# Attention on one Trainium2 core: the third tile's exponentials multiplied by ScalarE instead of VectorE

## The chip, the core and the metric

The kernel runs on one core of one Trainium2 chip. A core has engines that work side by side, each through a queue of its own in order: TensorE (PE in the profile, with its weight loads as PEld), VectorE (DVE), ScalarE (ACT), GpSimd (POOL) and SyncE (SP), which here issues the loads. The time is the device time of one execution in microseconds (us). Three executions of the kernel before took 1632.38 to 1636.96 us, with a median of 1633.7 us.

## The reference

The kernel computes a two-layer transformer block in float32 on 256 latent tokens and 256 context tokens of width 1024: a half feed-forward, a mixer and another half feed-forward in each layer. The first layer's mixer is attention with 8 query heads and 2 key and value heads of width 128, the second layer's is an mLSTM. The change touches the attention alone:

```python
def gqa_softmax(q, k, v):
    s = jnp.einsum('bqhgd,bkhd->bhgqk', q, k).astype(jnp.float32) * (ATT_HEAD_DIM ** -0.5)
    p = jax.nn.softmax(s, axis=-1).astype(v.dtype)
    return jnp.einsum('bhgqk,bkhd->bqhgd', p, v)
...
    k_all = jnp.concatenate([kl, kc], axis=1)
    v_all = jnp.concatenate([vl, vc], axis=1)
    ...
    ob = lax.map(lambda qblk: gqa_softmax(qblk, k_all, v_all), qb)
    ...
        oc = gqa_softmax(qc.reshape(B, Lc, ATT_KV_HEADS, ATT_GROUP, ATT_HEAD_DIM), kc, vc)
```

Latent queries see all 512 keys; context queries see the 256 context keys only. The softmax divides each row of exponentials by its sum. That division is what the change moves.

## The kernel before

All products of float32 are made from split operands. `split` (line 223) makes a high part by a cast on ScalarE (line 224) and a low part by a subtraction on VectorE (line 229), and `mm3` (line 238) makes three matmuls of them, high by high, high by low and low by high (line 240). So nearly everything that PE multiplies has passed ScalarE and then VectorE.

The program runs stage after stage: the first feed-forward, attention, the second feed-forward, the second layer's feed-forward, the mLSTM and the last feed-forward. In `attention` (line 932) the queries, keys and values are first projected (`part`, with the matmuls of lines 926 to 928), normalised (`evac`, line 956) and turned by transposes on PE (`turn`, line 975). Then a loop of 24 sub-steps runs over the 8 heads and three tiles of a head (line 1128). Tiles 0 and 1 are 128 latent queries each against all 512 keys. Tile 2, the "third tile", holds both blocks of 128 context queries, each against 256 keys, side by side in one tile of 128x512. In each sub-step `scores` makes the scores on PE, a minimum of each row on VectorE (line 1021; the query gain carries a minus sign, so it serves as the maximum), the exponentials with their sums on ScalarE (line 1024), the reciprocals of the sums on VectorE (line 1028), and the product of exponentials and reciprocals (lines 1029 to 1034). Tiles 0 and 1 have one exponential and one product of 128x512 each; the third tile has two of 128x256.

```python
                V.reciprocal(rs, sm)
                for j in range(n):
                    ej = e[:, j * w_ : (j + 1) * w_]
                    if SCALE[i] == "scalar":
                        S.activation(ej, ej, AF.Copy, scale=rs[:, j : j + 1])
                    else:
                        getattr(nc, SCALE[i]).tensor_scalar(ej, ej, rs[:, j : j + 1], None, ALU.mult)
```

`SCALE` (line 69) names the engine for each of the three tiles; before, it is GpSimd, VectorE and VectorE. Three sub-steps later (`AHEAD`, line 61) `values` (line 1037) transposes the scaled tile on PE in four blocks into PSUM (line 1041), splits the transposed tile, and, with the third tile, makes the head's product with the values and splits that as well. The PSUM tiles of these transposes come from a pool of two, which the splits set free. Query heads are split a head ahead (`queries`, line 1004). Between sub-steps `rest` (line 1117) and the loop's end put in the remaining query projections of the context tokens, turns of query blocks (lines 983 to 998), the weights of the output projection, and from sub-step 20 on its first products (`mix_unit`, line 900, with its sum on line 915).

The order of the instructions in each engine's queue is not that of the program text. A planner sets it when the program is built, from the dependencies, the free buffers, the place in the text as priority, and a time that it assumes for each instruction. Only instructions under `pin` keep their order among each other, such as the transposes of lines 983 and 1041. Once built, the queues are fixed and run in order.

## Time and profile before

| what | us |
|---|---|
| median of three executions | 1633.7 |
| lowest and highest | 1632.38, 1636.96 |
| the profiled execution, whole | 1633.42 |
| the profiled execution, its span | 1631.6 |
| attention's sub-steps, first exponential to last | 452 to 520 |
| PE, VectorE, ScalarE, GpSimd busy over the span | 1610.0, 1350.8, 748.9, 62.0 |

The span runs from the first to the last instruction of the profiled execution; the rest of its time lies around it. A row of a group gives the line, engine, operation and shapes, the number of instructions, their busy time and mean duration in nanoseconds, and the idle time of the engine just before them with what ended it. A row of the order in time gives the start and the duration in microseconds, how many instructions of one kind were merged, and in brackets the idle time before and its releaser. Ends of matmuls are modelled, so that a PE shown as busy is not PE at its peak.

### The profile page before, as it was taken

Reading aid. Unit: us, or ns where it says so; the run is one execution under the profiler, and the core shown is the slowest. Engines: PE = TensorE matmul, PEld = TensorE weight load, DVE = VectorE, ACT = ScalarE, POOL = GpSimd, SP = SyncE. Lnnn points to the kernel's source line nnn. Section 1 sums busy time; section 2 is a strip of 40 time slices with the busy share of each in tenths; the row PEclk is TensorE's granted clock in tenths of the full one; section 3 lists DMA queues with packets and bytes.
Section 4 is the critical chain, followed back from the end, with each engine's and each line's share of the span. In section 5 each row is a group of like instructions: output and inputs, shape, how many; then the busy total and the mean of one; then the engine's idle time right before and its main releaser. Section 6 shows DMA issues by size and latency. Waiting matters only on the chain. (4 is left out here: it accounts for less than half of the span.)

```text
span 1631.6 us, 26590 instructions
## 1 busy us (share of the span) xinstructions
PE 1610.0 (99%) x10308; PEld 1448.8 (89%) x10308; DVE 1350.8 (83%) x2689; ACT 748.9 (46%) x1273; POOL 62.0 (4%) x76
## 2 busy tenths in 40 slices
PE   9999999999999999999999999999999999999998
PEld 6888888889988998889998998889999989999987
DVE  5899977739889879899986979789966968897687
ACT  5622122314676453316662434236652657566542
POOL 0000000001011100000000100000001000020000
PEclk9999999999999999999999999999999999999999
DMA  9677765422202347633345248723362332427552
GB/s 367 220 233 244 239 200 194 142 78 85 65 1 76 145 134 219 220 125 104 121 148 184 78 157 286 249 66 120 104 223 100 98 130 84 145 100 258 181 177 91
DMA packets 72495, 252.59 MB, mean 155 GB/s; under 512 B 7984, under 2 KB 10800, under 8 KB 72368
## 3 DMA queue, kind: packets, MB, share of 16 engines
q1 hardware_dynamic: 71792, 250.10, 46.5%
q8 instruction: 81, 1.33, 0.3%
q10 hardware_dynamic: 576, 0.79, 0.1%
q14 instruction: 46, 0.38, 0.1%
HBM read 249.81 MB, written 1.05 MB: 154 GB/s over the span
## 5 line engine op out<-in xcount | busy, mean ns | idle before, releaser
L240 PE MATMUL t<-t,t 128*128 128x256 f32 (+2 forms) x8412 | 1316.5, 317 | 6.4 <-ACT t L224 3.3
L240 PEld LDWEIGHTS t<-t,t 128*128 128x128 f32 x8412 | 1185.2, 188 | 125.6 <-ACT t L224 5.0
L224 ACT CAST t<-t 128x1024 fp32r<-128x1024 f32 (+3 forms) x521 | 428.6, 844 | 488.9 <-PE t L240 215.8
L229 DVE TENSOR_TENSOR t<-t,t 128x256 fp32r<-128x256 f32 (+2 forms) x740 | 514.0, 729 | 114.1 <-ACT t L224 108.0
L340 DVE SCALAR_TENSOR_TENSOR t<-t,t 128x1024 bf16<-128x1024 f32 x224 | 260.7, 1220 | 0.0
L578 ACT ACTIVATE t<-t 128x512 f32<-128x512 f32 (+1 forms) x71 | 34.4, 489 | 107.1 <-PE t L240 107.1
L926 PE MATMUL t<-t,t 128*128 128x256 f32 (+1 forms) x256 | 79.3, 310 | 0.0
L708 DVE SCALAR_TENSOR_TENSOR t<-t,t,t 128x256 f32<-128x256 f32 x96 | 42.7, 478 | 43.9 <-PE t L240 43.6
L927 PE MATMUL t<-t,t 128*128 128x256 f32 (+1 forms) x256 | 78.4, 306 | 0.1
L928 PE MATMUL t<-t,t 128*128 128x256 f32 (+1 forms) x256 | 78.5, 307 | 0.0
L579 DVE TENSOR_TENSOR t<-t,t 128x512 f32<-128x512 f32 (+1 forms) x71 | 39.0, 553 | 44.1 <-PE t L240 30.8
L474 POOL TENSOR_TENSOR t<-t,t 128x256 f32<-128x256 f32 x30 | 23.3, 775 | 1111.4 <-ACT t L464 1110.0
L1441 PE MATMUL t<-t,t 128*128 128x512 f32 (+3 forms) x286 | 60.4, 366 | 1.7 <-ACT t L1518 1.0
L854 PE MATMUL t<-t,t 128*128 128x512 f32 (+1 forms) x300 | 60.5, 364 | 0.0
L1441 PEld LDWEIGHTS t<-t,t 128*128 128x128 f32 (+2 forms) x286 | 43.7, 159 | 18.6 <-issue 2.8
L854 PEld LDWEIGHTS t<-t,t 128*128 128x128 f32 x300 | 51.5, 189 | 8.9
L464 ACT ACTIVATE t<-t 128x256 f32<-128x256 f32 x72 | 26.1, 412 | 65.6 <-DVE t L457 65.6
L927 PEld LDWEIGHTS t<-t,t 128*128 128x128 f32 x256 | 48.1, 188 | 3.3 <-DVE t L229 0.8
L926 PEld LDWEIGHTS t<-t,t 128*128 128x128 f32 x256 | 48.3, 189 | 2.7
L928 PEld LDWEIGHTS t<-t,t 128*128 128x128 f32 x256 | 48.1, 188 | 2.5
L631 DVE TENSOR_TENSOR t<-t,t 128x512 f32<-128x512 f32 x66 | 45.3, 687 | 0.4
L531 ACT ACTIVATE t<-t,t 128x256 fp32r<-128x256 f32 x72 | 32.8, 503 | 27.7 <-DVE t L530 27.7
(201 smaller groups left out, 1069.5 us busy)
## 6 DMA issues: line engine op xcount, KB each, us to landing
t<-in_ffn_in SPq DMA_DIRECT2D x168, 512.0 KB, 4.0
t<-in_ada_w SPq DMA_DIRECT2D x137, 512.0 KB, 4.3
t<-in_ffn_out SPq DMA_DIRECT2D x66, 512.0 KB, 4.4
t<-in_ffn_last SPq DMA_DIRECT2D x22, 512.0 KB, 3.5
t<-in_att_in SPq DMA_DIRECT2D x12, 512.0 KB, 3.5
t<-in_c SPq DMA_DIRECT2D x8, 512.0 KB, 8.0
t<-in_att_out SPq DMA_DIRECT2D x8, 512.0 KB, 3.6
t<-in_ml_qk SPq DMA_DIRECT2D x8, 512.0 KB, 3.8
```

The costliest lines, as they stand in the source:

```text
L224: self.behind(self.nc.scalar.copy(h, x))
L229: self.behind(self.nc.vector.tensor_tensor(out=ls, in0=xs, in1=hs.bitcast(F32), op=ALU.subtract))
L240: mm = lambda *k, **kw: self.nc.tensor.matmul(*k, skip_group_check=not group, **kw)
L340: ins = nc.vector.scalar_tensor_tensor(self.tmp().bitcast(BF16), r, 1.0, self.cb[:, v, :], ALU.mult, ALU.mult, accum_out=to)
L579: V.tensor_tensor(out=sl, in0=sl, in1=pu[:, :n], op=ALU.mult)
L631: add = lambda o, x, y: V.tensor_tensor(out=o, in0=x, in1=y, op=ALU.add)
L708: V.scalar_tensor_tensor(z, y[:, gg[0] - t0 : gg[1] - t0], gate()[:, v, d : d + 1], z, ALU.mult, ALU.add)
L854: pin(nc.tensor.matmul(o, gs[g], ws[k][w][:, i : i + n], start=k == k0 and g == w == 0, stop=k == k1 - 1 and g == 1,))
L926: mm(o, self.xh[:, k, c], wh, start=k == 0, stop=False)
L927: mm(o, self.xh[:, k, c], wl, start=False, stop=False)
L928: mm(o, self.xl[:, k, c], wh, start=False, stop=k == ND - 1)
L1441: mm = lambda *k, **kw: pin(nc.tensor.matmul(*k, **kw))
```

## The change

For the third tile of each head, ScalarE's copy with a scale takes the place of VectorE's multiplication by a scalar: sixteen instructions of 128x256, two to each of eight heads. They read the same exponentials, take the same reciprocals and write to the same place. The branch for it is in `scores` already (line 1031), so that one constant is all that differs:

```diff
@@ -66,7 +66,7 @@
 APD = (4, 5, 6, 7)
 APA = (0, 1, 2, 3, 4, 5, 6, 7)
 QB = 2
-SCALE = ('gpsimd', 'vector', 'vector')
+SCALE = ('gpsimd', 'vector', 'scalar')
 FINE = 4
 FINE0 = 1
```

## The prediction

> **What bounds the kernel now.** I read the head of the page first, then the stretches of the attention stage, then the groups of that stage by shape, and at last the engines' own rows in order of time around each head. From the page, the span and the busy shares:

> ```profile
> span 1631.6 us, 26590 instructions
> PE 1610.0 (99%) x10308; PEld 1448.8 (89%) x10308; DVE 1350.8 (83%) x2689; ACT 748.9 (46%) x1273; POOL 62.0 (4%) x76
> ```

> PE is busy for 99% of the span, so over the whole kernel little but PE's own work sets the time. The change touches one stage only. The stretches of ten microseconds there (columns: length, then busy time and instructions of PE, PEld, DVE, ACT, POOL, then clock, DMA share, GB/s):

> ```profile
> 460.00:470.00 10.00, 8.84 (x67) 8.05 (x66) 9.11 (x25) 6.37 (x20) 1.56 (x1) 1.00 0.00 1
> 480.00:490.00 10.00, 8.37 (x57) 6.95 (x56) 9.54 (x21) 6.55 (x16) 3.12 (x2) 1.00 0.00 0
> 490.00:500.00 10.00, 8.23 (x65) 7.67 (x63) 9.17 (x22) 7.19 (x20) 1.57 (x1) 1.00 0.01 2
> 500.00:510.00 10.00, 8.93 (x60) 7.83 (x59) 9.68 (x21) 7.28 (x18) 1.57 (x1) 1.00 0.31 103
> 510.00:520.00 10.00, 10.00 (x60) 8.75 (x60) 9.13 (x18) 6.20 (x14) 1.57 (x1) 1.00 0.34 109
> ```

> From 460 to 510 VectorE is busy for 9.1 to 9.7 of every 10 us, ScalarE for 6.4 to 7.3, and PE is short of full; from 510 on PE is full. So up to 510 VectorE looks like the limit, and afterwards PE is. How much PE loses is in the groups of the stretch 455 to 531 (last columns: idle time before them, and who ended it):

> ```profile
> L240 PE MATMUL t<-t,t 128*128 128x256 f32 x186 | 27.8, 288 | 4.3 <-ACT t L224 3.1 <-DVE t L229 1.2
> L1041 PE MATMUL t<-t,t 128*128 128x128 f32 x96 | 14.6, 275 | 2.0 <-DVE t L229 1.7 <-ACT t L998 0.2
> L224 ACT CAST t<-t 128x512 fp32r<-128x512 f32 x37 | 21.2, 598 | 14.3 <-PE t L1041 8.7 <-PE t L240 5.6
> L1024 ACT ACTIVATE t<-t,t 128x256 f32<-128x256 f32 x16 | 7.5, 476 | 4.7 <-DVE t L1021 4.7
> ```

> PE stands idle for 4.3 + 2.0 = 6.3 us in these groups. That bounds any ordinary gain: not 0.4% of the time. The first two rows also say that VectorE, though the fuller queue, is not the only one that PE waits for: 3.1 + 0.2 us end with ScalarE (the high part of a split, line 224, or line 998), 1.2 + 1.7 us with VectorE (the low part, line 229). The third row shows ScalarE waiting for PE in turn. It is a round trip, PE (scores or transposes) to ScalarE (high part) to VectorE (low part) to PE, and a delay on either engine counts if it lies on it.

> **The change, part by part.** *Removed from VectorE.* The 16 multiplications of the third tiles, two to each of 8 heads:

> ```profile
> L1034 DVE TENSOR_SCALAR t<-t,t x24: 342/348/489, 455.9 to 520.1; 128x256 f32<-128x256 f32 x16, 128x512 f32<-128x512 f32 x8
> 478.45 0.61 DVE L1034 TENSOR_SCALAR t<-t,t 128x256 f32<-128x256 f32 x2
> 478.97 0.68 DVE L229 TENSOR_TENSOR t<-t,t 128x512 fp32r<-128x512 f32 x1
> ```

> One takes about 0.35 us, and the pair holds the queue for 478.97 - 478.45 = 0.52 us, up to its whole length of 0.61. I take 0.55: 8 x 0.55 = 4.4 us of VectorE's queue. It counts where PE's idle time ends with a subtraction that stood behind a pair:

> ```profile
> 461.35 1.79 PE L240 MATMUL t<-t,t 128*128 128x256 f32 x12 [1.16 <-DVE t L229]
> 462.38 0.61 DVE L1034 TENSOR_SCALAR t<-t,t 128x256 f32<-128x256 f32 x2
> 485.15 0.61 DVE L1034 TENSOR_SCALAR t<-t,t 128x256 f32<-128x256 f32 x2
> 487.43 0.63 PE L1041 MATMUL t<-t,t 128*128 128x128 f32 x4 [0.62 <-DVE t L229]
> 501.25 0.60 DVE L1034 TENSOR_SCALAR t<-t,t 128x256 f32<-128x256 f32 x2
> 503.16 0.66 PE L1041 MATMUL t<-t,t 128*128 128x128 f32 x4 [1.07 <-DVE t L229]
> ```

> The 1.16 us at 461.35 lie ahead of the first pair (462.38) and stay. At 487.43 and 503.16 a pair stands about two microseconds before, and each gives at most its 0.55: together -1.1 us.

> *Added to ScalarE.* Sixteen copies with a scale that is a column of its own, 128x256. The trace of before has none of that very form. The nearest is line 554, also 128x256 with a column operand (its bias):

> ```profile
> L554 ACT ACTIVATE t<-t,t x64: 492/501/515, 422.7 to 1476.7; 128x256 f32<-128x256 f32 x64
> 447.61 1.71 ACT L554 ACTIVATE t<-t,t 128x256 f32<-128x256 f32 x4
> L551 ACT ACTIVATE t<-t x16: 400/402/412, 18.0 to 59.0; 128x256 f32<-128x256 f32 x16
> ```

> One takes 0.50 us; four take 1.71, so they follow each other at (1.71 - 0.50) / 3 = 0.40. The copy without a column operand (line 551) takes 0.40 alone, which is the lower end; I take line 554's, as the operands are alike. A pair holds ScalarE for 0.80 us, 8 pairs for 6.4 us. [...]

> No table of functions has to be loaded for the copies: the copies of line 971 already run between the exponentials, with a single load of 1.28 us ahead of the first exponential.

> ```profile
> 449.81 1.28 ACT L1024 ACT_TABLE_LOAD   x1
> 452.83 2.17 ACT L971 ACTIVATE t<-t,t 128x128 f32<-128x128 f32 x8
> ```

> The copies can start only when VectorE's reciprocal is done, and ScalarE takes its queue in order: behind them stand the casts of line 224, for which PE waits. Where ScalarE stood idle just behind a head's exponentials, the copies are covered; elsewhere they push the next cast. The rows that decide, heads counted from 0:

> ```profile
> 461.72 0.17 DVE L1028 RECIPROCAL t<-t 128x2 f32<-128x2 f32 x1
> 463.61 0.59 ACT L224 CAST t<-t 128x512 fp32r<-128x512 f32 x1
> 464.25 0.30 PEld L240 LDWEIGHTS t<-t,t 128*128 128x128 f32 x2 [0.18 <-ACT t L224]
> 480.57 0.66 PE L1041 MATMUL t<-t,t 128*128 128x128 f32 x4 [0.20 <-ACT t L998]
> 485.24 0.59 ACT L224 CAST t<-t 128x512 fp32r<-128x512 f32 x1 [0.24 <-PE t L240]
> 488.74 1.29 PE L240 MATMUL t<-t,t 128*128 128x256 f32 x5 [0.68 <-ACT t L224]
> 493.37 0.16 DVE L1028 RECIPROCAL t<-t 128x2 f32<-128x2 f32 x1
> 494.01 1.07 ACT L224 CAST t<-t 128x512 fp32r<-128x512 f32 x2 [0.69 <-PE t L240]
> 496.29 0.61 PE L240 MATMUL t<-t,t 128*128 128x256 f32 x2 [1.77 <-ACT t L224]
> 500.35 0.20 ACT L1024 ACTIVATION_READ_ACCUMULATOR t<-t,t 128x1 f32 x1
> 500.44 1.07 ACT L224 CAST t<-t 128x512 fp32r<-128x512 f32 x2
> 500.58 0.17 DVE L1028 RECIPROCAL t<-t 128x2 f32<-128x2 f32 x1 [0.15 <-ACT t L1024]
> 508.36 0.20 ACT L1024 ACTIVATION_READ_ACCUMULATOR t<-t,t 128x1 f32 x1
> 508.93 0.15 DVE L1028 RECIPROCAL t<-t 128x2 f32<-128x2 f32 x1
> 509.58 2.97 ACT L224 CAST t<-t 128x512 fp32r<-128x512 f32 x4 [1.02 <-PE t L240]
> ```

> Head 0: the copies come ahead of the cast at 463.61, which had no idle time before it and which the weight load at 464.25 waits for: +0.80. Head 2: the same ahead of line 998, which ends PE's 0.20 at 480.57: +0.80. Head 3: the cast at 485.24 has 0.24 us to give, and the chain from it ends PE's wait at 488.74: +0.56. Head 4: ScalarE is idle from the reciprocal's end, 493.53, to 494.01, so 0.48 are covered, and the casts lead to PE's wait of 1.77 at 496.29: +0.32. Head 5: nothing is idle at 500.44, and the chain ends in the wait at 503.16: +0.80. Together +3.3 us. Head 1 falls into 464 to 472, where PE has the query projections of lines 926 to 928 between the heads' own work; heads 6 and 7 fall behind 508, where PE runs on without a wait (10.00 in the stretch from 510). I cost those three at nothing; without that cover head 1 costs 0.80 and head 6, with 0.50 free at 509.08 to 509.58, costs 0.30, and head 7 about as much.

> *What else moves.* The tile that is scaled is transposed up to three sub-steps later, so its own lateness reaches PE last; I cost it at nothing. No DMA, no PSUM buffer and no PE instruction changes. GpSimd keeps the first tiles. The order of each queue is planned when the program is built, from the engines' assumed costs, and will be planned anew; the trace of before cannot show how. Its price is bounded below by the 6.3 us that PE idles here and above by the case in which each pair is paid in full.

> **Sum:** +3.3 - 1.1 = +2.2 us. The profiled execution took 1633.42 us, 1.8 more than its span, and 0.3 less than the median of 1633.7 that the result is compared with. I put the sum on the median: 1635.9, 0.13% up. The bound for telling a difference is 0.3%, 4.9 us; the likeliest result is therefore "within 0.3%".

> **Rivals.** *ScalarE's order becomes the limit (slower).* If the copies stand in front of the casts in every head and the queue also waits for the reciprocal, a head costs 0.80 plus that wait. At head 6 the last exponential's sum is there at 508.56 and the reciprocal at 509.08, 0.52 later; at head 5 at 500.55 and 500.75, 0.20 later. So 1.0 to 1.3 us a head, 8.0 to 10.4 in all: 1642 to 1644. For it: PE's waits end with ScalarE a little more often, 3.3 against 2.9 us, and a head then has more on ScalarE than on PE. Against it: the 14.3 us that the casts idle, waiting for PE. It decides from 4.9 / 8 = 0.6 us net a head.

> *VectorE is the limit (faster).* Then the stage follows its queue: -4.4 us, 1629.3, and the reduces of line 1021, for which the exponentials of the third tiles alone wait 4.7 us, come earlier as well. Going past 0.3% takes more than the 4.4 and most of the 6.3 us of PE's idle time: about -5.5, 1628.2. For it: 9.68 of 10 busy. Against it: ScalarE pays 6.4 for VectorE's 4.4, in the same round trip, and from 510 PE is the limit.

> *Nothing moves.* Both are hidden, because the scaled tile is needed three sub-steps later: 1633.7, within a microsecond. For it: PE has other sub-steps' matmuls queued. Against it: the five waits above.

> **How the numbers follow.** Within 0.3%, my sum and the hidden case together: 0.45. ScalarE's order, or a new plan that leaves PE waiting: 0.40; a queue in order with a round trip inside tends to cost more than a sum of single waits shows. Faster than 0.3%: 0.15, as it needs nearly all of PE's idle time. The range goes from 1628.5, VectorE's whole 4.4 and a little of the reduces' lateness, to 1644, ScalarE's upper end; the likeliest case's own range is 1629 to 1638.6.

> **What would show it.** In the profile after, 16 copies of 0.50 us on ScalarE under line 1032 and none of 128x256 left on VectorE; VectorE lower by about 0.7 us in each stretch of ten (4.4 over some 62), ScalarE higher by about 1.0; the waits of PE for line 224 longer and those for line 229 shorter between 464 and 503; the same time behind the attention stage. I am wrong if PE's idle time in 455 to 531 falls from 6.3 to 2 or less, if it grows past 11, or if the difference in time arises in another stage, which would mean that the new order and not the two prices decides.

## The result, and the profile after

The changed kernel took 1640.9 us (median of 11 executions, 1636.64 to 1643.44), the kernel before 1634.04 in the same comparison (11 executions, 1632.38 to 1637.44). The ratio is 1.003, with a 95% interval of 1.0022 to 1.0038: slower by 4.9 us (3.6 to 6.2). The ratio goes by the means, which lie 5.0 us apart; the medians lie 6.9 apart. Repeated beside other kernels, the ratio was 1.0039 (1.0024 to 1.0054). That lies on the bound of 0.3% that the prediction drew between "no change" and "slower": small, but clear of the noise.

The page of the kernel after, its span and busy shares:

```profile
span 1639.4 us, 26584 instructions
PE 1614.5 (98%) x10308; PEld 1453.5 (89%) x10308; DVE 1346.6 (82%) x2673; ACT 754.9 (46%) x1289; POOL 62.2 (4%) x76
```

VectorE lost 4.2 us of work (1350.8 to 1346.6) and ScalarE got 6.0 (748.9 to 754.9), as a table of prices would have it. PE did the same 10308 matmuls but was busy 4.5 us longer, and the span grew by 7.8. The growth is mostly in the attention. The exponentials of line 1024 in the kernel before, and then in the kernel after (engine, operation, count; least, median and greatest ns; first and last start):

```profile
L1024 ACT ACTIVATE t<-t,t x32: 463/591/737, 452.2 to 519.1; 128x512 f32<-128x512 f32 x16, 128x256 f32<-128x256 f32 x16
```

```profile
L1024 ACT ACTIVATE t<-t,t x32: 463/594/737, 452.0 to 524.6; 128x512 f32<-128x512 f32 x16, 128x256 f32<-128x256 f32 x16
```

From the first to the last exponential it was 66.9 us and is 72.6: 5.7 more. The last transposes of line 1041 start at 529.2 and 535.1, so 5.9 of the 7.8 us have come by then. The other 1.9 arise behind the attention, where both kernels run the same instructions in the same order; the last section comes back to them. The kernel after, its groups by shape in the stretch 455 to 531, and the new copies by line:

```profile
L240 PE MATMUL t<-t,t 128*128 128x256 f32 x173 | 28.2, 304 | 4.4 <-ACT t L224 3.2 <-DVE t L229 1.2
L224 ACT CAST t<-t 128x512 fp32r<-128x512 f32 x35 | 20.3, 600 | 16.3 <-PE t L1041 13.8 <-PE t L240 2.5
L1041 PE MATMUL t<-t,t 128*128 128x128 f32 x88 | 14.3, 283 | 2.9 <-DVE t L229 2.1 <-ACT t L998 0.8
L1024 ACT ACTIVATE t<-t,t 128x256 f32<-128x256 f32 x16 | 7.5, 476 | 4.3 <-DVE t L1021 4.3
L983 PE MATMUL t<-t,t 128*128 128x128 f32 x16 | 3.3, 297 | 1.8 <-ACT t L971 1.8
```

```profile
L1032 ACT ACTIVATE t<-t,t x16: 492/510/548, 462.7 to 525.8; 128x256 f32<-128x256 f32 x16
```

PE's idle time in these groups is 4.4 + 2.9 + 1.8 = 9.1 us, where it was 6.3. (By 531 the kernel after has made only 88 of its 96 transposes; counted to 540, with all of them in both kernels, it is 9.4 against 6.6.) A wait has come that was not there at all, for line 971 (1.8). And the same matmul has become dearer: line 240 takes 304 ns at 128x256 where it took 288. Why that is, the stretches of ten show (columns as in the prediction; before first, one stretch that was not shown there, then after):

```profile
470.00:480.00 10.00, 9.94 (x74) 8.90 (x74) 8.81 (x27) 7.68 (x22) 1.57 (x1) 1.00 0.01 2
```

```profile
470.00:480.00 10.00, 8.19 (x66) 7.68 (x65) 7.66 (x23) 7.86 (x21) 1.57 (x1) 1.00 0.01 2
480.00:490.00 10.00, 9.22 (x49) 8.32 (x50) 6.48 (x14) 7.70 (x21) 1.56 (x1) 0.66 0.00 0
500.00:510.00 10.00, 7.45 (x47) 6.50 (x46) 8.11 (x16) 8.24 (x19) 3.09 (x2) 0.89 0.08 13
510.00:520.00 10.00, 10.00 (x55) 8.65 (x54) 6.91 (x14) 6.02 (x13) 1.21 (x1) 0.94 0.31 97
```

From 470 to 480 PE falls from 9.94 to 8.19. In the next stretch it looks busier than before (9.22 against 8.37) and yet does less (49 instructions against 57), because its granted clock is 0.66. VectorE is no longer at 9.1 to 9.7 but at 6.5 to 8.1 in these rows: it waits now.

**The first loss, step by step.** ScalarE in the kernel before and then in the kernel after, in order of time, around the end of head 1 and the first exponential of head 2:

```profile
469.21 0.71 ACT L998 ACTIVATE t<-t,t 128x512 f32<-128x512 f32 x1
469.79 0.70 ACT L1024 ACTIVATE t<-t,t 128x512 f32<-128x512 f32 x1
478.10 1.17 ACT L971 ACTIVATE t<-t,t 128x128 f32<-128x128 f32 x4
```

```profile
469.17 0.92 ACT L1032 ACTIVATE t<-t,t 128x256 f32<-128x256 f32 x2
469.98 0.69 ACT L998 ACTIVATE t<-t,t 128x512 f32<-128x512 f32 x1
470.55 0.70 ACT L1024 ACTIVATE t<-t,t 128x512 f32<-128x512 f32 x1
478.79 0.91 ACT L1032 ACTIVATE t<-t,t 128x256 f32<-128x256 f32 x2 [0.23 <-DVE t L1028]
479.60 1.12 ACT L971 ACTIVATE t<-t,t 128x128 f32<-128x128 f32 x4
```

The pair holds ScalarE from 469.17 to 469.98, 0.81 us, and the next head's exponential is 0.76 later. VectorE waits for it. VectorE before and after:

```profile
469.56 0.61 DVE L1034 TENSOR_SCALAR t<-t,t 128x256 f32<-128x256 f32 x2
470.62 0.16 DVE L1028 RECIPROCAL t<-t 128x1 f32<-128x1 f32 x1 [0.46 <-ACT t L1024]
477.65 0.16 DVE L267 SCALAR_TENSOR_TENSOR t<-t,t 128x4 f32<-128x4 f32 x1
```

```profile
471.37 0.16 DVE L1028 RECIPROCAL t<-t 128x1 f32<-128x1 f32 x1 [1.77 <-ACT t L1024]
478.67 0.67 DVE L1021 TENSOR_REDUCE t<-t 128x1 f32<-128x512 f32 x1
479.25 0.15 DVE L267 SCALAR_TENSOR_TENSOR t<-t,t 128x4 f32<-128x4 f32 x1
```

The multiplications that were taken off VectorE stood in a hole: without them its wait for this exponential is 1.77 instead of 0.46, and its next work starts 0.75 later than before. Line 267 ends the chain that scales the next query block; it comes 1.60 later, partly by that delay and partly because the planner has put a row minimum (478.67) ahead of it. Line 971 waits for it and stands behind head 2's own copies besides. PE has nothing else left. PE after, in order of time:

```profile
480.00 0.33 PE L983 MATMUL t<-t,t 128*128 128x128 f32 x1 [1.81 <-ACT t L971]
482.32 1.11 PE L1041 MATMUL t<-t,t 128*128 128x128 f32 x4 [0.78 <-ACT t L998]
498.97 0.84 PE L240 MATMUL t<-t,t 128*128 128x256 f32 x3 [1.73 <-ACT t L224]
506.87 0.63 PE L1041 MATMUL t<-t,t 128*128 128x128 f32 x4 [2.08 <-DVE t L229]
507.97 7.32 PE L240 MATMUL t<-t,t 128*128 128x256 f32 x33 [0.47 <-ACT t L224]
```

The clock falls right behind the first and the fourth of these waits. Stretches of 1 us of the kernel after:

```profile
479.00:480.00 1.00, 0.00 (x1) 0.00 (x1) 0.41 (x2) 1.00 (x4) 0.00 (x0) 1.00 0.00 0
481.00:482.00 1.00, 0.55 (x3) 0.14 (x1) 0.58 (x2) 0.80 (x3) 0.25 (x1) 0.50 0.00 0
486.00:487.00 1.00, 1.00 (x7) 1.00 (x6) 0.40 (x2) 0.00 (x0) 0.00 (x0) 0.50 0.00 0
505.00:506.00 1.00, 0.00 (x0) 0.00 (x0) 0.63 (x2) 1.00 (x4) 0.30 (x1) 1.00 0.00 0
510.00:511.00 1.00, 1.00 (x6) 0.94 (x5) 1.00 (x3) 0.16 (x1) 0.00 (x0) 0.50 0.90 369
```

From 480.5 to 487.3 and again from about 507.8 to 511.2 PE ran at half clock. The kernel before had 1.00 in all of its stretches there, and its same 33 matmuls took 5.87 us, not 7.32:

```profile
503.67 5.87 PE L240 MATMUL t<-t,t 128*128 128x256 f32 x33
```

### The profile page after: what moved, and what is told of

It is laid out like the page before. It is cut to its first block, busy times and chain, and to the rows that moved or that the text cites. A ratio compares the mean times of both kernels' runs of the same rounds, so it can differ in the third digit from the quotient of the medians.

```text
span 1639.4 us, 26584 instructions
## 1 busy us (share of the span) xinstructions
PE 1614.5 (98%) x10308; PEld 1453.5 (89%) x10308; DVE 1346.6 (82%) x2673; ACT 754.9 (46%) x1289; POOL 62.2 (4%) x76
## 3 DMA queue, kind: packets, MB, share of 16 engines
HBM read 249.81 MB, written 1.05 MB: 153 GB/s over the span
## 5 line engine op out<-in xcount | busy, mean ns | idle before, releaser
L240 PE MATMUL t<-t,t 128*128 128x256 f32 (+2 forms) x8412 | 1321.2, 318 | 7.0 <-ACT t L224 3.4
L240 PEld LDWEIGHTS t<-t,t 128*128 128x128 f32 x8412 | 1189.4, 189 | 125.7 <-ACT t L224 4.8
L224 ACT CAST t<-t 128x1024 fp32r<-128x1024 f32 (+3 forms) x521 | 428.9, 844 | 494.1 <-PE t L240 206.2
L229 DVE TENSOR_TENSOR t<-t,t 128x256 fp32r<-128x256 f32 (+2 forms) x740 | 513.5, 727 | 116.1 <-ACT t L224 111.7
```

What stands on the lines that cost most here:

```text
L224: self.behind(self.nc.scalar.copy(h, x))
L229: self.behind(self.nc.vector.tensor_tensor(out=ls, in0=xs, in1=hs.bitcast(F32), op=ALU.subtract))
L240: mm = lambda *k, **kw: self.nc.tensor.matmul(*k, skip_group_check=not group, **kw)
```

## Experiments

The theory after the result was: ScalarE's copies delay what stands behind them in ScalarE's queue, and PE's wait for line 971 is the chief place of it. The rivals were the planner's new order of line 267, the clock alone, and VectorE's relief as something that counts. All ratios are to the kernel before in the same comparison.

One table serves several of the experiments. It gives how late the second exponential of each head's third tile starts, in us, counted from the first exponential of all and less the same in the profile of the kernel before. Each line is one profiled execution and holds its drops of the clock; the last column counts them between 450 and 540 us, in steps of 3.4 us at half clock.

| kernel | head 0 | 1 | 2 | 3 | 4 | 5 | 6 | 7 | half-clock steps |
|---|---|---|---|---|---|---|---|---|---|
| after | 0.0 | 0.1 | 1.0 | 1.9 | 3.5 | 3.0 | 3.5 | 5.7 | 3 |
| after, again | -0.1 | 0.0 | 0.8 | 1.9 | 3.3 | 2.8 | 3.3 | 5.4 | 3 |
| before, again | 0.0 | 0.0 | 1.1 | 1.1 | 1.1 | 1.1 | 1.2 | 1.2 | 1 |
| multiplications left out | 0.0 | -0.5 | 1.0 | 0.9 | 0.7 | 0.8 | -0.3 | 0.3 | 1 |
| copies added | -0.1 | 0.0 | 2.1 | 2.4 | 5.3 | 4.7 | 3.7 | 5.5 | 3 |
| head 2 alone | -0.1 | -0.1 | 1.0 | 1.7 | 1.8 | 1.8 | 1.8 | 1.8 | 1 |
| order of line 267 alone | 0.0 | 0.0 | 0.0 | -0.4 | 0.5 | 0.8 | 0.8 | 0.8 | 0 |
| order repaired | 0.0 | 0.1 | 3.0 | 2.6 | 3.6 | 4.1 | 5.2 | 5.9 | 2 |
| heads 0 and 1 alone | -0.1 | 0.0 | 0.8 | 1.0 | 3.1 | 3.4 | 3.4 | 3.4 | 2 |
| heads 2 to 7 alone | 0.0 | 0.0 | 0.0 | 0.7 | 0.6 | 0.1 | 0.5 | 2.4 | 1 |

**Both kernels once more.** No edit.

> The kernel before, once more, to see how its granted clock and its time go together. Theory A (the clock: PE's waits in the attention became long enough that TensorE's clock is granted less for a few microseconds, and that is most of the difference) expects a clock of 0.998 to 0.999 in its executions, with no stretch of the attention under 0.95, and within this one program a longer time where the mean clock is lower, by about 1.6 us for each 0.001. Theory B (the queues: the copies push the casts behind them, 0.8 us for a pair, and the clock is beside the point) expects the 4 us that lie between executions of the same program to have nothing to do with the clock.

> The kernel after, once more: the queues are the same from run to run, so only the clock can differ. Theory A expects the executions to fall in groups by their mean clock: near 1637 to 1638 at 0.998 to 0.999 and near 1641 at 0.994 to 0.995. Theory B expects times that do not follow the clock, and the same idle times of PE with the same total in each.

Before: 1.0006 (0.9997 to 1.0016). After: 1.0039 (1.0024 to 1.0054), with the same waits and the same two half-clock stretches of the attention in its profile. The kernel before brought something of its own: with unchanged queues its clock was below 1.00 twice.

```profile
460.00:470.00 10.00, 8.88 (x57) 8.38 (x58) 9.05 (x24) 6.03 (x19) 1.56 (x1) 0.83 0.00 0
930.00:940.00 10.00, 10.00 (x74) 9.95 (x74) 7.36 (x24) 3.39 (x10) 0.00 (x0) 0.85 0.24 78
```

Ten microseconds at 0.83 are 1.7 us of full clock lost, and the table shows what that costs here: 1.1 us from head 2 on, to the end. So a difference of about a microsecond between two profiles says nothing on its own.

**Head 2's pair left on VectorE** (against after):

```diff
-                    if SCALE[i] == "scalar":
+                    if SCALE[i] == "scalar" and hd != 2:
...
-                        getattr(nc, SCALE[i]).tensor_scalar(ej, ej, rs[:, j : j + 1], None, ALU.mult)
+                        getattr(nc, SCALE[i if hd != 2 else min(i, 1)]).tensor_scalar(ej, ej, rs[:, j : j + 1], None, ALU.mult)
```

> The changed kernel with the third tile of head 2 given back to VectorE, the one whose pair of copies stands in front of line 971 and behind which PE waits 1.81 us at 480. Theory A expects that wait to fall under 1 us, the stretch 480 to 490 back at a clock of 1.00, and 2 to 4 us off the changed kernel: about 1637. Theory B expects one eighth of the difference: about 1640.

1.0035 (1.0023 to 1.0047), no gain, and PE's wait for line 971 is longer than with the pair:

```profile
480.31 0.33 PE L983 MATMUL t<-t,t 128*128 128x128 f32 x1 [2.29 <-ACT t L971]
```

The idea that head 2's copies, which stand directly ahead of line 971, cause that wait falls.

**Copies a sub-step later in the program's text** (against after), so that the planner gives them a lower priority:

```diff
-                        S.activation(ej, ej, AF.Copy, scale=rs[:, j : j + 1])
+                        behind.append((3 * hd + i + 1, lambda ej=ej, r=rs[:, j : j + 1]: S.activation(ej, ej, AF.Copy, scale=r)))
...
-            es, pt = [], []
+            es, pt, behind = [], [], []
...
-                rest(n)
+                rest(n), [f() for at, f in behind if at == n]
```

> The changed kernel with the two copies issued at the end of the next sub-step, and so later in the planner's priority; they still come before the transposes that read them. ScalarE's work is the same, VectorE's too. Theory A expects a time that goes with the longest waits of PE: if none in 470 to 515 is over 1 us, a clock of 1.00 there and 1634 to 1636. Theory B expects the copies to come behind the casts more often and so most of the 3.3 us of the prediction's loss gone while VectorE's relief stays: about 1633, whatever the clock does.

1.0026 (1.0017 to 1.0036). The wait at 480 is down to 0.27, and others have come. PE in order of time:

```profile
482.47 0.83 PE L1041 MATMUL t<-t,t 128*128 128x128 f32 x4 [0.88 <-ACT t L1032]
484.52 0.85 PE L240 MATMUL t<-t,t 128*128 128x256 f32 x3 [1.23 <-ACT t L224]
506.47 5.78 PE L240 MATMUL t<-t,t 128*128 128x256 f32 x24 [1.65 <-ACT t L224]
```

Put late, the copies themselves keep the transposes waiting (the first row), which the prediction had costed at nothing.

**The third tile's multiplications left out** (against after), VectorE's relief without ScalarE's load:

```diff
-                for j in range(n):
+                for j in range(n if i < 2 else 0):
```

> The kernel before with the third tiles not multiplied by their reciprocals at all (the softmax of the context queries stays unnormalised): VectorE loses 4.4 us of queue and ScalarE gains nothing. The prediction's sum expects 1.1 us less than before, about 1633; VectorE as the limit of the stage expects the whole 4.4 us, about 1629.6; the reading that the round trip and not VectorE's fullness sets the stage expects no difference that can be told.

0.9993 (0.9983 to 1.0002): -1.1 us (-2.8 to +0.3). Taking 4.4 us of work from the engine that is busiest after PE brings about a quarter of it, and the interval allows nothing at all; it does not allow the 4.4.

**The copies added, VectorE's multiplications kept** (against before), ScalarE's load without VectorE's relief:

```diff
-                        getattr(nc, SCALE[i]).tensor_scalar(ej, ej, rs[:, j : j + 1], None, ALU.mult)
+                        getattr(nc, SCALE[i]).tensor_scalar(ej, ej, rs[:, j : j + 1], None, ALU.mult); i == 2 and S.activation(t([P, TL], tag="spare", bufs=2), ej, AF.Copy, scale=rs[:, j : j + 1])
```

> The kernel before with VectorE's multiplications left in place and, behind each of a third tile, ScalarE's copy of 128x256 into a spare tile that nobody reads: ScalarE's 6.4 us of added queue alone. The prediction's sum expects 3.3 us more than before, about 1637.3. If nearly all of the changed kernel's difference is what ScalarE's queue does to PE's waits and to the clock, it expects 4 to 7 us more, with PE's idle time in the attention up by 2 us or more and the clock under 0.95 somewhere in 475 to 515. If the difference comes from the new order of PE's queue, it expects under 2 us, as far as the order stays that of before.

1.0022 (1.0011 to 1.0032): +3.6 us (1.8 to 5.2). These copies write to a tile of their own and start only behind VectorE's multiplications, so they are not quite the copies of the change. The same wait stands at the same place, and the stretch from 485 to 490 ran at a clock of 0.55:

```profile
481.51 0.33 PE L983 MATMUL t<-t,t 128*128 128x128 f32 x1 [2.04 <-ACT t L971]
```

The two halves together make 3.6 - 1.1 = +2.5 us, against 4.9 for the whole. The difference of 2.4 carries an uncertainty of about 2.7 (the three intervals' half-widths 1.3, 1.55 and 1.7, by squares), so it is not shown that the halves interact.

**GpSimd in ScalarE's place** (against after):

```diff
-SCALE = ('gpsimd', 'vector', 'scalar')
+SCALE = ('gpsimd', 'vector', 'gpsimd')
```

> The third tile's multiplications on GpSimd in place of VectorE or ScalarE: VectorE's relief of 4.4 us without ScalarE's load, on an engine that takes 1.57 us for the first tile's 128x512. If the relief of VectorE is worth its 1.1 us and GpSimd's time is covered by the three sub-steps, 1633, that is no difference that can be told; a version that beats both kernels would have to show under 1629.

1.0013 (1.0003 to 1.0022), +2.1 us (0.5 to 3.6). Better than ScalarE, but no gain on before. Its profiled execution was 0.8 late at head 7, with one half-clock step, and had the highest wait of PE, 1.56 us, at 503.67. But it was the fastest of its ten (1633.29), no slower than the profiled one of before, so it can't show where the 2.1 us lie: that stays open.

**Only head 2's pair moved** (against after):

```diff
-                    if SCALE[i] == "scalar":
+                    if SCALE[i] == "scalar" and hd == 2:
...
-                        getattr(nc, SCALE[i]).tensor_scalar(ej, ej, rs[:, j : j + 1], None, ALU.mult)
+                        getattr(nc, SCALE[i if hd == 2 else min(i, 1)]).tensor_scalar(ej, ej, rs[:, j : j + 1], None, ALU.mult)
```

> The kernel before with one pair alone, that of head 2, moved to ScalarE. PE's queue stays word for word that of before, and the copies stand behind line 971 in ScalarE's queue, not in front of it. The queue's price expects 0.80 us less what VectorE gives back, so 0 to 0.8 us over before and line 971 as early as before, with no new wait of PE over 1 us; if one pair by itself opens a wait and takes the clock with it, 2 to 4 us over before.

1.0002 (0.9993 to 1.0012): +0.3 us (-1.1 to +2.0): one pair alone brings no difference that can be told, and its price of 0.80 lies in the interval too. PE's queue is the same as before. The expectation of no new wait over 1 us was missed: PE's 0.20 for line 998 has become 1.27. PE in order of time:

```profile
481.52 0.66 PE L1041 MATMUL t<-t,t 128*128 128x128 f32 x4 [1.27 <-ACT t L998]
```

In the table this execution is 1.0 late at head 2, about what one half-clock step costs in "before, again" (1.1), and 1.7 to 1.8 from head 3 on. So some 0.7 us come behind head 2's pair, and they stay to the end of the stage.

**The order of line 267 alone** (against before): the engines as before, but line 267 tied behind the next row minimum, as the planner has it in the changed kernel.

```diff
-                r = self.rsqrt(ss, len(tts) * n, RMS_EPS, 1.0 / P)
+                r = self.rsqrt(ss, len(tts) * n, RMS_EPS, 1.0 / P, lambda ins: setattr(self, "chain", ins))
...
-                V.tensor_reduce(mx, s.rearrange("p (n f) -> p n f", n=n), AX.X, ALU.min)
+                low = V.tensor_reduce(mx, s.rearrange("p (n f) -> p n f", n=n), AX.X, ALU.min); (hd, i) == (3, 0) and self.tc.add_manual_dep(self.chain.ins, low.ins.name, mybir.DependencyInfo(mybir.DependencyClass.NoSync, mybir.DependencyReason.DATA), reason="chain")
```

> The kernel before, all engines as before, with one edge for the planner: the last step of the norm's rsqrt in front of line 971 (line 267, context queries of the second block) stands behind the row minimum of the next head, as it does in the changed kernel. No work is added or taken away. If the new order of the queues is what opens PE's wait at 478 to 480, this kernel has a wait of PE of 1.5 us or more for line 971 there, a clock under 0.8 behind it in most executions, and 1.5 to 4 us more than before. If ScalarE's added work is the cause, nothing that can be told.

1.0002 (0.9993 to 1.0011): +0.3 us (-1.1 to +1.8). PE in order of time:

```profile
479.88 0.33 PE L983 MATMUL t<-t,t 128*128 128x128 f32 x1 [0.91 <-ACT t L971]
482.11 0.66 PE L1041 MATMUL t<-t,t 128*128 128x128 f32 x4 [1.02 <-ACT t L998]
```

That one change of order makes half of the wait of 1.81, and the clock stayed at 1.00 in the attention.

**The changed kernel with that order repaired** (against after): the reverse tie, the row minima of head 2's third tile and of head 3's first behind line 267. `rsqrt` passes the chain's last instruction on as above.

```diff
+                low = V.tensor_reduce(mx, s.rearrange("p (n f) -> p n f", n=n), AX.X, ALU.min); (hd, i) in ((2, 2), (3, 0)) and self.tc.add_manual_dep(low.ins, self.chain.ins.name, mybir.DependencyInfo(mybir.DependencyClass.NoSync, mybir.DependencyReason.DATA), reason="chain")
```

> The changed kernel with the opposite edge: the row minima of the two sub-steps behind that rsqrt wait for it, so that line 971 comes ahead of the exponentials and the copies. All 16 copies stay on ScalarE. If the order is the cause, the wait at 480 falls under 0.5 us, the clock there is 1.00, and 1.5 to 4 us of the changed kernel's difference go: 1635 to 1638. If ScalarE's work is the cause, it stays within 1 us of the changed kernel, about 1640.

1.0033 (1.002 to 1.0046), +5.4 us (3.3 to 7.5): no gain. PE in order of time:

```profile
479.65 0.33 PE L983 MATMUL t<-t,t 128*128 128x128 f32 x1 [0.90 <-ACT t L971]
482.31 0.83 PE L1041 MATMUL t<-t,t 128*128 128x128 f32 x4 [1.55 <-ACT t L1032]
484.36 1.01 PE L240 MATMUL t<-t,t 128*128 128x256 f32 x2 [1.22 <-ACT t L224]
```

The wait for line 971 is halved, and what was gained stands two and four microseconds later, as waits for the copies and for the cast behind them. With the run before it: the planner's order of line 267 is not the cause by itself. The lateness here is ScalarE's, and that order says only at which row PE meets it. The planner changed more than this one place: PE's own queue in the kernel after differs from that of before between 463 and 520. No run has all sixteen copies with the old order, so what the rest of the new order costs was not tested. Two runs bear on it: head 2's pair cost its 0.7 us with PE's queue unchanged, and with the multiplications left out PE's queue was new from 461 on and nothing was lost.

**Heads 2 to 7 alone, and heads 0 and 1 alone** (against after; the second with `(0, 1)`):

```diff
-                    if SCALE[i] == "scalar":
+                    if SCALE[i] == "scalar" and hd in (2, 3, 4, 5, 6, 7):
...
-                        getattr(nc, SCALE[i]).tensor_scalar(ej, ej, rs[:, j : j + 1], None, ALU.mult)
+                        getattr(nc, SCALE[i if hd in (2, 3, 4, 5, 6, 7) else min(i, 1)]).tensor_scalar(ej, ej, rs[:, j : j + 1], None, ALU.mult)
```

> Six of the eight pairs on ScalarE, those of heads 0 and 1 left on VectorE. PE's queue is that of before up to head 3, near 483. The order as the cause expects no new wait at 480 and a clock of 1.00 from 475 to 490, and about half of the changed kernel's difference left, from the later heads: 1636 to 1638. The load as the cause expects six eighths of it: 1639.

> Only the pairs of heads 0 and 1 on ScalarE. The planner's order up to line 971 of the second context block is then that of the changed kernel, though no copy stands near it. The order as the cause expects a wait of PE of 1.5 us or more at 478 to 481, a clock under 0.8 behind it, and 2 to 4 us over before: about 1637. The load as the cause expects two eighths of the difference: about 1635.5.

Heads 2 to 7: 1.002 (1.0011 to 1.003), +3.3 us (1.8 to 4.9). Heads 0 and 1: 1.0018 (1.0009 to 1.0027), +2.9 us (1.5 to 4.4). They add up to 6.2, beside 4.9 and 6.4 for the whole in its two comparisons. So the loss has two places, and two of the eight heads hold about half of it, within intervals of 1.5 us to either side. Heads 2 to 7 alone, VectorE and then PE:

```profile
471.02 0.17 DVE L1028 RECIPROCAL t<-t 128x1 f32<-128x1 f32 x1 [0.46 <-ACT t L1024]
```

```profile
504.52 0.85 PE L1041 MATMUL t<-t,t 128*128 128x128 f32 x4 [2.10 <-DVE t L229]
```

Heads 0 and 1 alone, VectorE and then PE:

```profile
470.79 0.16 DVE L1028 RECIPROCAL t<-t 128x1 f32<-128x1 f32 x1 [1.77 <-ACT t L1024]
```

```profile
479.85 0.48 PE L983 MATMUL t<-t,t 128*128 128x128 f32 x1 [2.29 <-ACT t L971]
```

Without the first two heads' copies VectorE's wait is the 0.46 of before, the table has no lateness at head 2 and little up to head 6, and the loss comes at head 7, behind the wait of 2.10. With them alone VectorE waits 1.77, PE 2.29, and all of the 3.4 has come by head 5, two half-clock steps included. These are single executions: at their ends they were 5.4 and 2.0 us later than the profiled one of before, and not 2.4 and 3.4.

## Why the prediction was right or wrong

The forecast of 1635.9 was 5.0 us below the measured 1640.9. The whole range held it; the likeliest case's own range, up to 1638.6, did not, and the case "within 0.3%" is only just at its edge. The direction and both prices were right, the sum was less than half of what it should have been.

**VectorE's relief, -1.1.** Right in size: -1.1 measured, with the multiplications left out, though the interval (-2.8 to +0.3) makes the close agreement luck. The rows bear it out by half: without the multiplications PE's wait of 0.62 at 487 is gone, but the other, 1.07 at 503, is not shorter (1.39). And as the kernel after shows, at head 1 the pair stood in a hole, where its removal brings nothing.

**ScalarE's copies, +3.3 in all.** As a sum right: +3.6 (1.8 to 5.2) for the copies alone. The single price of 0.50 came out at 0.51 (median of sixteen), the pair's 0.80 at 0.81, and no table was loaded between exponentials and copies: the only load from 448 to 543 us is the one of 1.28 us at 449.62, ahead of the first exponential. Head by head about half of it was wrong:

- Head 0, +0.80: not seen. The weight load's 0.18 is gone, another of 0.22 waits for the copies at 463.25, and head 1's exponentials were on time (0.1 late).
- Head 1, nothing, "PE has the query projections": **this is the step that failed.** The projections do cover PE from 464 to 472, but not ScalarE's queue. The copies push head 2's first exponential by 0.76, VectorE waits for it, and PE, which was full from 470 to 480 (9.94), runs dry when the projections are spent: 1.81. The cover delayed the wait by 8 us, and I had taken delay for removal. The prediction named 0.80 as the price without the cover; heads 0 and 1 together measured 2.9 (1.5 to 4.4); they were not taken apart, but nothing was late before head 1's pair.
- Head 2, +0.80: seen where the pair moves without heads 0 and 1. PE's 0.20 became 1.27, alone and with heads 2 to 7, and some 0.7 us came behind it. In the kernel after it is covered by head 1's loss: the wait there, 1.81 + 0.78, also stands without head 2's pair (2.29 + 0.78).
- Head 3, +0.56: not seen. PE's wait of 0.62 for line 229 and of 0.68 for line 224 have gone down to one of 0.32.
- Head 4, +0.32: not seen, 1.77 before and 1.73 after.
- Head 5, +0.80 less the relief: the wait of 1.07 became 2.08, a little more than the copies hold ScalarE for. The pair at 503.75 to 504.56 stands ahead of the next exponential and of the casts (505.23) that PE's wait leads back to, by way of the subtraction at 506.04. Right place, right mechanism; but the half-clock step behind it (507.8 to 511.2) was not in the sum.
- Heads 6 and 7, nothing: right. From 510 on PE is at 10.00.

**The planner's new order.** The prediction bounded it by PE's idle time of 6.3 us for a gain and by the pairs paid in full for a loss, and the result lies between. PE's idle time in 455 to 531 grew from 6.3 to 9.1 us; the sign of being wrong, more than 11, did not come. The order of line 267 costs nothing that could be measured (+0.3), and putting it right brought nothing; the rest of the new order was not tested by itself.

**The clock, taken as constant.** This is the term that was missing. Mean granted clock over the executions for which it is on record was 0.9978 before (91 executions) and 0.9960 after (15). Within one and the same kernel an execution is 0.9 us longer for each 0.001 that its mean clock is lower (202 executions of all kernels, each kernel with a mean of its own; the clock accounts for 42% of their scatter). So 1.8 x 0.9 = 1.6 us of the mean difference of 5.4 goes with the clock. The executions with a mean clock of at least 0.998 agree: 1637.9 us after (5) against 1634.4 before (60), still 3.5 apart. That leaves 3.5 to 3.8 us for the waits, against a forecast of 2.2. The split is rough: the mean clock is recorded to 0.001, and it takes in a stretch at half clock that ends every profile, some 4 to 7 us by a clock of 0.95 to 0.91 from 1600 to 1640.

**"The same time behind the attention."** On the mean I can't say; in the profiled pair 1.9 of the 7.8 us arose later, but with the same instructions in the same order, and the kernel before shows such shifts against itself.

**VectorE's 0.7 less and ScalarE's 1.0 more in each ten.** Right over the span (4.2 and 6.0 us), not readable by stretches, since the whole stage has been drawn out: VectorE shows 6.48 instead of 9.54 from 480 to 490, because it waits.

**The rivals.** "VectorE is the limit" is refuted by the multiplications left out: -1.1 (-2.8 to +0.3) and not -4.4. VectorE was at 9.1 to 9.7 of 10, and still the move to ScalarE cost 4.9 us. "Nothing moves" is refuted by the interval. "ScalarE's order becomes the limit" was nearer to the truth than the forecast: its condition, more than 0.6 us net a head, is just what came out on the mean (4.9 / 8 = 0.6). But it put the loss evenly on eight heads with a wait for the reciprocal in each; the copies after waited only 0.7 us for reciprocals in all sixteen, and most of the loss sits at two places. The tendency named with its chance, that a queue in order with a round trip inside costs more than a sum of single waits, was my estimate; here the whole cost 4.9 us where the sum gave 2.2.

## What to carry to other kernels

A busy engine's work may stand in its holes: before moving it, look in the order of time whether the engine waits right behind it. Here, with the pair gone, VectorE's wait for the next exponential went from 0.46 to 1.77 us, and the relief was worth nothing there. On the receiving engine, ask what stands behind the new instruction in the queue, and follow that one around the whole round trip to the end of PE's stock of other work; here a cover that lasted to 478 put the wait off by 8 us and did not take its 1.81 us away. And where PE's waits grow, count the granted clock behind them as a term of its own, here 1.6 us of the mean difference of 5.4.

## What the runs showed of the hardware

The clock fell in steps. In every profiled execution the loss between 450 and 540 was 0, 1.7, 3.4 or 5.1 us (one less the granted clock, times the length), that is 3.4 us at half clock, once, twice or three times. The kernel before had none in one profile and one in the other, the kernel after three in both. The length of the waits does not decide it: the kernel before stood a wait of 1.77 us at 496 without a drop, and its two profiles, with the same queues and the same wait of 1.16 us at 461, differ in just this. In the first, shown in the prediction, the twelve matmuls behind that wait took 1.79 us; the second, PE in order of time, has

```profile
461.12 2.48 PE L240 MATMUL t<-t,t 128*128 128x256 f32 x12 [1.16 <-DVE t L229]
```

Nor is it bound to the change. Of the 1.9 us that the profiled execution of the kernel after lost behind the attention, most came in this stretch, with the clock below 1.00 behind a wait of 1.02 us at 932 that the kernel before has too (1.05 at 927, and its clock stayed at 1.00):

```profile
930.00:940.00 10.00, 8.98 (x62) 8.72 (x61) 7.27 (x25) 2.74 (x9) 1.63 (x2) 0.83 0.37 116
```

PE was not idle in the steps ahead of these drops: in the kernel after it was busy for 0.47 of the step before 480.50 and for 0.30 of the one before 507.80. No wait of PE in the attention was longer than 2.29 us in any of the profiles, and drops stood behind waits of 1.02 us (at 932 in the kernel after), 1.16 (at 461 in the second profile of before), 1.81 and 2.08 (at 480 and 507 in the kernel after). That such a wait causes the drop was not tested by itself. And behind the attention the share of a step does not tell it: the drop at 934.47 followed a step with 0.70. In two profiles (head 2's pair alone, heads 2 to 7 alone) the clock was 0.99 from 1300 to 1600 as well; where in that stretch it fell is not shown.
